# An encoder layer with product-key experts on one core: a second buffer and a shorter period for the seven-product key pairs, attention bias and mask laid out in DRAM, weight splits shared out anew, and another order of the last norm

## The chip, the cores and the metric

The kernel runs on one core of a Trainium2 chip. The metric is device time in microseconds (us) of one execution; the lower the better. Three runs of the kernel before took 979.08, 978.34 and 982.81 us, median 979.08 us. A profile was taken of one more execution.

Engines: PE (TensorE) multiplies matrices out of SBUF into PSUM; DVE (VectorE) and POOL (GpSimd) do elementwise arithmetic; ACT (ScalarE) does activations and copies with a scale; SP (SyncE) issues most DMAs. Each works through its own instructions in a fixed order and waits on semaphores.

## The reference, cut to what matters

One encoder layer on x of 256 tokens by 1024, all in float32:

```
h   = rmsnorm(x) * (1 + sc1) + sh1
[q,k,v | q,k,v] = h @ w_in                    two groups of 8 heads of 64
group A: 2-D neighbourhood attention, learned bias na_rpb, window of 16 columns
group B: three dilated windows, bias -slope[head] * distance, merged by their softmax sums
x   = x + g1 * concat(rmsnorm(oA), rmsnorm(oB)) @ w_out
h2  = rmsnorm(x) * (1 + sc2) + sh2
PEER(h2): q = h2 @ wq; the 16 best of 128 x 128 keys for each of 8 heads, gates = softmax
          y = sum over the chosen (i, j) of gate * gelu(h2 . u[i, j]) * v[i, j]
out = rmsnorm(x + g2 * PEER(h2))
```

u and v are 128 x 128 experts of 1024 numbers: 64 MB each. sh, sc, g come from a product of silu(c) with ada_w.

## The kernel before, in words

**Splits.** A float32 product is made as three products of fp32r parts: a weight tile `raw` (128 x 1024, 512 KB) is loaded by SP (L87), ACT copies its high part `hi` (L96), and DVE or POOL subtracts to get the low part `lo` (L97); then hi·hi, hi·lo and lo·hi are accumulated on PE (`mm3`, L138 to L141). The list `order` (L103 to L120) holds all weight tiles in the order of use, each with a letter: "b" puts its `lo` on POOL, "c" on DVE, "s" is a pair's half that is already in SBUF. `unit()` (L126) hands out the next tile and splits `lead` tiles ahead. `raw`, `hi` and `lo` have a few buffers each, so a load waits until an old tile is used up. WI and WO are the letters of the last eight w_in tiles and of the eight w_out tiles.

**Stages.** (1) Norm, modulation, and the first q, k, v (to about 73 us). (2) Attention (L565 to L596): twelve steps; step i runs one weight tile (V of group B, q and k of group B, then w_out of group A), the scores of head pair i (`att_scores`, L421), the turned probabilities of pair i-1 (`att_turn`) and the values of pair i-2 (`att_values`, L459). For each head and half of the tokens DVE adds the bias and takes the minimum (`st`, L442), ACT takes the exponential (L444), and PE turns it (`pTp`, L453) and multiplies with v (`op`, L466). The bias of group A, `e2s`, is loaded and masked on DVE (L579); that of group B, `dls`, is made from two rows by ACT (L549) and POOL (L550) under the table DLS. Between these DVE sums the modulation (`araw`, L217, `ADA` tells how many pairs of tiles in a step), and at the end w_out of group B and the second norm follow. (3) The queries wq, the scores and the best keys (to about 325 us). (4) `u_chunk` (L661): a tile of u, 24 matmuls of 256 columns, and a Gelu; 36 chunks (AHEAD) while the routing is made, then BESIDE = 92 beside the 64 steps that build the gates (`gp`, L851; `jm` and `gi` on DVE); HOLD is how many of these are left for the last step. (5) The v loop (L1013): for each key i the gated column (`gated`, L879: ACT and DVE write `wx`) times the tile v[i], 4 x 3 matmuls of 512 columns into four PSUM banks `yp`. (6) The last norm (L1045 to L1070).

**Seven products.** Two keys i, i+1 whose index is in `seven` (L115) are taken as one pair: the eight block products (2 keys x 2 halves of tokens x 2 halves of columns) become seven, by Strassen's way in Winograd's form. For that DVE makes sums of the gates (`pair_s`, L928: `sr`, `sx`) and of the weights (`pair_t13`, `pair_t24`, L915 to L922), and splits them (`pair_split`, L924: `sph`, `spl`). `todo` (L1009) says how many places of `plan` ahead of the pair each is done. A pair takes one place of `plan`, so with a distance of 8 keys (SEVEN) there are 6 single keys and a pair in a period. The pair's two raw tiles sit in one buffer `bb` inside GA. At the end `fold` (L997) adds the shared sums to the result.

**What sets the order.** The program is written in the order of the code above, but the order on each engine and on SP's queue is set by the tool that schedules it by its own costs and the buffers; `issue_after` (here on L574, L1062) pins an instruction behind another.

## Time and profile before

| | us |
|---|---|
| median of three runs | 979.08 |
| the profiled execution | 980.62 |
| its span, first to last instruction | 978.8 |
| PE busy | 952.0 |
| DVE busy | 783.5 |
| ACT busy | 565.5 |
| POOL busy | 451.2 |
| from about 74 us to 173 us (attention and second norm) | 99 |
| v loop, first matmul to last | 628.7 to 970.2 |
| last matmul to the end of the span | 8.6 |

The span leaves out 1.8 us of the execution's time. A matmul's busy time is modelled and overlaps the next one's, so PE's busy share says less than the idle times that the timeline puts in brackets, with what ended them. TensorE's clock has two levels, 1.2 and 2.4 GHz; a stretch of the table of windows shows the mean granted, 1.00 being 2.4 GHz.

### The profile page before, as it was taken

What the parts mean: (1) busy time and instruction counts of PE and PEld (TensorE: products, weight loads), DVE (VectorE), ACT (ScalarE), POOL (GpSimd) and SP (SyncE); (2) the same over time, 40 slices, a digit from 0 to 9 for tenths busy, and PEclk for the clock granted to TensorE, in tenths of its full rate; (3) what the DMA queues carried; (4) which work ended last, traced back from release to release, by engine and by line L of the source; (5) the groups of instructions that cost most, each with busy time, mean ns of one, the idle gap of its engine ahead of it and who ended that gap; (6) DMA issues with size and microseconds to landing.
All of it is one profiled execution on the core that took longest, in us unless ns stands there. A gap on an engine that the chain in (4) does not pass through costs nothing.

```text
span 978.8 us, 17367 instructions
## 1 busy us (share of the span) xinstructions
PE 952.0 (97%) x6292; PEld 867.9 (89%) x6292; DVE 783.5 (80%) x1800; ACT 565.5 (58%) x1043; POOL 451.2 (46%) x201
## 2 busy tenths in 40 slices
PE   8899998999999999999999999899999999999996
PEld 5787888999999999999999999888888888888885
DVE  6859888899992677788889887667787888887786
ACT  4366576645445666666666665454655665665653
POOL 2678457677888677777777776300000000000002
PEclk8999799999999999999999999999999999999998
DMA  9776784555554455555545555578657666656562
GB/s 349 284 262 252 260 304 160 160 173 161 184 184 141 152 165 162 170 159 165 164 161 172 155 170 156 177 268 309 222 183 261 235 200 205 195 192 209 158 206 73
DMA packets 53398, 193.76 MB, mean 198 GB/s; under 512 B 5816, under 2 KB 6080, under 8 KB 53184
## 3 DMA queue, kind: packets, MB, share of 16 engines
q1 hardware_dynamic: 52672, 191.59, 59.4%
q8 instruction: 49, 0.80, 0.3%
q10 hardware_dynamic: 576, 1.05, 0.3%
q14 instruction: 37, 0.30, 0.1%
q0 software_dynamic: 64, 0.01, 0.0%
HBM read 190.52 MB, written 2.11 MB: 197 GB/s over the span
## 4 chain that ended last, share of the span: by engine, by line
PE 83%; DVE 3%; issue 2%; ACT 1%; POOL 1%; POOLq 0%; ACTq 0%; DVEq 0%
PE ps L139 15%; PE ps L140 14%; PE ps L141 14%; PE y L140 10%; PE y L139 10%; PE y L141 10%; PE gp L851 3%; PE P L140 1%; DVE araw L217 1%; PE P L139 1%; PE P L141 1%; PE op L466 1%; PE scp L706 1%; ACT hi L96 1%; PE pTp L453 0%
## 5 line engine op out<-in xcount | busy, mean ns | idle before, releaser
L97 POOL TENSOR_TENSOR lo<-raw,hi 128x1024 fp32r<-128x1024 f32 x172 | 422.4, 2459 | 159.1 <-PE ps L141 73.5
L96 ACT ACTIVATE hi<-raw 128x1024 fp32r<-128x1024 f32 x282 | 297.2, 1057 | 187.5 <-issue 63.2
L139 PE MATMUL ps<-h2h,hi 128*128 128x256 f32 x1128 | 320.5, 285 | 3.0 <-DVE GB L868 2.6
L140 PE MATMUL ps<-h2l,hi 128*128 128x256 f32 x1128 | 319.0, 283 | 0.0
L141 PE MATMUL ps<-h2h,lo 128*128 128x256 f32 x1128 | 318.8, 283 | 0.0
L139 PEld LDWEIGHTS ps<-h2h,hi 128*128 128x128 f32 x1128 | 216.2, 192 | 4.1 <-DVE GB L868 3.0
L140 PEld LDWEIGHTS ps<-h2l,hi 128*128 128x128 f32 x1128 | 216.4, 192 | 0.0
L141 PEld LDWEIGHTS ps<-h2h,lo 128*128 128x128 f32 x1128 | 216.2, 192 | 0.0
L97 DVE TENSOR_TENSOR lo<-raw,hi 128x1024 fp32r<-128x1024 f32 x110 | 134.7, 1225 | 53.8 <-issue 44.3
L140 PE MATMUL y<-lo,wx 128*128 128x512 f32 x424 | 165.1, 389 | 0.0
L141 PE MATMUL y<-hi,wx 128*128 128x512 f32 x424 | 165.1, 389 | 0.0
L139 PE MATMUL y<-hi,wx 128*128 128x512 f32 x424 | 165.1, 389 | 0.0
L837 DVE SCALAR_TENSOR_TENSOR gi<-iotaG,iT,gT 128x256 fp32r<-128x256 f32 x256 | 113.8, 476 | 30.5 <-PE gp L851 30.5
L1063 POOL TENSOR_TENSOR GB<-GB 128x512 f32<-128x512 f32 x2 | 2.6, 1290 | 258.3 <-ACT GB L1056 258.3
L141 PEld LDWEIGHTS y<-hi,wx 128*128 128x128 f32 x424 | 79.6, 188 | 16.8
L139 PEld LDWEIGHTS y<-hi,wx 128*128 128x128 f32 x424 | 79.6, 188 | 16.7
L140 PEld LDWEIGHTS y<-lo,wx 128*128 128x128 f32 x424 | 79.6, 188 | 16.5 <-DVE lo L97 0.3
L854 DVE TENSOR_TENSOR gp<-gp,gl 128x512 f32<-128x512 f32 x64 | 44.6, 697 | 8.3 <-ACT gl L853 6.7
L883 ACT ACTIVATE wx<-GB 128x256 fp32r<-128x256 f32 x72 | 28.7, 411 | 36.5 <-PE y L141 36.1
L834 DVE TENSOR_TENSOR jm<-iotaG,jT 128x512 fp32r<-128x512 f32 x64 | 43.6, 681 | 1.6 <-ACT iotaG L823 1.6
L857 ACT ACTIVATE GB<-gp 128x368 f32<-128x368 f32 (+31 forms) x64 | 21.3, 332 | 37.4 <-DVE gp L854 37.4
L989 POOL DMA_DIRECT2D g2d<-g2r x1 | 0.6, 594 | 88.9 <-ACT wxh L943 88.9
(266 smaller groups left out, 1518.0 us busy)
## 6 DMA issues: line engine op xcount, KB each, us to landing
raw<-in_u SPq DMA_DIRECT2D x128, 512.0 KB, 3.5
raw<-in_v SPq DMA_DIRECT2D x106, 512.0 KB, 3.6
araw<-in_ada SPq DMA_DIRECT2D x20, 1024.0 KB, 5.7
raw<-in_w_in SPq DMA_DIRECT2D x24, 512.0 KB, 6.2
GA<-in_v SPq DMA_DIRECT2D x22, 512.0 KB, 4.4
...
```

Of the source, the lines that this page charges most:

```text
L96: nc.scalar.activation(hi, raw, AF.Copy)
L97: ins = eng.tensor_tensor(lo, raw, hi.bitcast(F32), op=OP.subtract)
L139: nc.tensor.matmul(ps, wh, ah, start=first, stop=False)
L140: nc.tensor.matmul(ps, wh, al, start=False, stop=False)
L141: return nc.tensor.matmul(ps, wl, ah, start=False, stop=last)
L217: block_sum.ins = nc.vector.tensor_tensor_reduce(raw, raw, silb, 1.0, init, OP.mult, OP.add, m).ins
L834: nc.vector.tensor_tensor(jm, iotaG[:, None, :].to_broadcast([128, 4, 128]), jT[:, t0:t0 + 4, None].to_broadcast([128, 4, 128]), op=OP.is_ ...
L837: nc.vector.scalar_tensor_tensor(gi[:, t, :, :], iotaG[:, None, :].to_broadcast([128, 2, 128]), iT[:, t0 + t:t0 + t + 1], gT.bitcast(F32)[ ...
L851: nc.tensor.matmul(gp[:, t, :, :], jm[:, t, :], gi[:, t, :, :], start=True, stop=True)
L854: nc.vector.tensor_tensor(gp[:, :, 0, :], gp[:, :, 0, :], gl, op=OP.add)
L857: nc.scalar.activation(GB[:, m:, t0:t0 + 4], gv[:, done:, :], AF.Copy)
L883: nc.scalar.activation(wh, w, AF.Copy)
```

## The change

- **Pairs**: SEVEN's distance goes from 8 keys to 6: 14 pairs for 11. The pair's raw tiles get two rooms in turn, the second one in GA's first cells. The gates' sums are made 4 places ahead (5 before), the weights' sums 3 and 2 (4 and 3 before).
- **u chunks**: BESIDE goes from 92 to 90 and HOLD from 3 to 1. The two chunks left (u[126], u[127]) are run inside the v loop, one behind v[0] and one behind v[1], and their `lo` is made on DVE.
- **Attention**: of the last eight w_in tiles and of the eight w_out tiles every second `lo` is made on DVE. Group B's bias is a table in DRAM of 128 x 3072 (1,536 KB in place of 384 KB), loaded straight into `dls` after step 2, so ACT's and POOL's eight instructions each fall away. Group A's table holds the mask already; DVE's subtraction from the mask becomes a change of sign on ACT. The copy of v's second half and the scaling of the values (`osb`) move from DVE to ACT (the latter in two instructions for one).
- **Last norm**: the gain goes into tiles of its own (`z`), all on DVE and in an order that `then` pins; POOL has only the two powers left. Of the four stores three leave on SP and one on ACT's queue.

```diff
--- before.py
+++ after.py
@@ -23,33 +23,29 @@
-BESIDE = 92
+BESIDE = 90
-HOLD = 3
-SEVEN = (31, 8, 112)
+HOLD = 1
+SEVEN = (31, 6, 112)
-FG0 = (("p", 0, 512), ("p", 512, 1024))
-FG1 = (("v", 0, 512), ("v", 512, 1024))
-SC0 = (("p", 512, 1024), ("a", 0, 512))
-SC1 = (("v", 0, 512), ("a", 512, 1024))
-DLS = (0, 0, 1, 1, 2, 2, 3, 3)
+DLAT = 2
-WI = 'bbbbbbbb'
+WI = 'bcbcbcbc'
-WO = 'bbbbbbbb'
+WO = 'bcbcbcbc'
...
@@ -116,7 +112,9 @@
         plan = [i for i in range(NKEY - LAST) if i - 1 not in seven]
         parts = []
         for i in plan:
-            order += [(p, "s") for p in range(2)] if i in seven else [(v[i], "c")]
+            order += [(seven.index(i) % 2 * 2 + p, "s") for p in range(2)] if i in seven else [(v[i], "c")]
+            if i < NKEY - AHEAD - BESIDE:
+                order.append((u[AHEAD + BESIDE + i], "c"))
         order += [(v[i], "c") for i in range(NKEY - LAST, NKEY)]
         ready = []
...
-                    nc.scalar.activation(v_s[g][:, 0, :], vps[g][0], AF.Copy)
-                    nc.vector.tensor_copy(v_s[g][:, 1, :], vps[g][1])
+                    for T in range(2):
+                        nc.scalar.activation(v_s[g][:, T, :], vps[g][T], AF.Copy)
                         nc.tensor.matmul(op[:, T, :], pts[:, b, T, :], v_s[g][:, b, h * HD:(h + 1) * HD],
-                nc.vector.tensor_tensor(osb[g][:, :, h * HD:(h + 1) * HD], op, ri[:, :, None].to_broadcast([128, 2, HD]),
-                                        op=OP.mult)
+                for T in range(2):
+                    nc.scalar.activation(osb[g][:, T, h * HD:(h + 1) * HD], op[:, T, :], AF.Copy, scale=ri[:, T:T + 1])
...
-            dl = PA.tile([128, 2, 384], F32)
-            nc.sync.dma_start(dl, dil.rearrange("p (a s) -> p a s", a=2))
-            def bias_head(h):
-                nc.scalar.activation(dls[:, h, :], dl[:, 0, :], AF.Copy, scale=2.0 ** -(h + 1))
-                nc.gpsimd.tensor_add(dls[:, h, :], dls[:, h, :], dl[:, 1, :])
-                for h in range(NH):
-                    if DLS[h] == i:
-                        with tc.issue_after(split.pool):
-                            bias_head(h)
+                if i == DLAT:
+                    nc.sync.dma_start(dls, dil.rearrange("p (h s) -> p h s", h=NH))
-                    e3 = e2s[:, 2 * i:2 * i + 2].rearrange("p h s k -> p (h s) k")
-                    nc.vector.tensor_tensor(e3, mask[:, None, :].to_broadcast([128, 12, 64]), e3, op=OP.subtract)
+                    e3 = e2s[:, 2 * i:2 * i + 2].rearrange("p h s k -> p (h s k)")
+                    nc.scalar.activation(e3, e3, AF.Copy, scale=-1.0)
...
-            bb, bt = bl[:, 0:4, :], bl[:, 4:8, :]
-            parts += [bb[:, 3:4, :], bb[:, 0:3:2, :]]
+            bt = bl[:, 4:8, :]
+            rooms = [bl[:, 0:4, :], GA[:, 0:8, :].rearrange("p (b a) t -> p b (a t)", a=2)]
+            for bb in rooms:
+                parts += [bb[:, 3:4, :], bb[:, 0:3:2, :]]
             def pair_load(i):
+                bb = rooms[seven.index(i) % 2]
             def pair_t13(i):
+                bb = rooms[seven.index(i) % 2]
             def pair_t24(i):
+                bb = rooms[seven.index(i) % 2]
...
-                for d, f in ((6, pair_load), (5, pair_s), (4, pair_t13), (3, pair_t24),
+                for d, f in ((6, pair_load), (4, pair_s), (3, pair_t13), (2, pair_t24),
+                if done < NKEY:
+                    ps = u_chunk(done)
+                    nc.scalar.activation(ps[:, :S], ps[:, :S], AF.Gelu)
+                    nc.vector.tensor_mul(cell(done, 0, S), ps[:, :S], cell(done, 0, S))
+                    done += 1
...
+            z = [used(7 + T) for T in range(2)]
+            last = [None]
+            def then(do, *args, **kw):
+                with tc.issue_after(last[0]) if last[0] is not None else nullcontext():
+                    last[0] = do(*args, **kw).ins
+            def gain_of(n):
+                fs = slice(n % 2 * 512, (n % 2 + 1) * 512)
+                then(nc.vector.tensor_mul, z[n // 2][:, fs], ys[n // 2][:, fs], fgb[:, fs])
+            def mean(T):
+                then(nc.vector.tensor_scalar, m[:, T:T + 1], ssq[:, n:n + 1], ssq[:, n + 1:n + 2], EPS, op0=OP.add, op1=OP.add)
+            def scaled(T, f, eng, queue):
+                fs = slice(f * 512, (f + 1) * 512)
+                if eng == "a":
+                    nc.scalar.activation(z[T][:, fs], z[T][:, fs], AF.Copy, scale=r[:, T:T + 1])
+                else:
+                    then(nc.vector.tensor_scalar, z[T][:, fs], z[T][:, fs], r[:, T:T + 1], None, op0=OP.mult)
+                queue.dma_start(out[T * 128:(T + 1) * 128, fs], z[T][:, fs])
+            for n in range(4):
+                T, f = divmod(n, 2)
+                y, fs = ys[T], slice(f * 512, (f + 1) * 512)
+                then(nc.vector.tensor_tensor, y[:, fs], yp[T][f], g2b[:, fs], op=OP.mult)
+                then(nc.vector.tensor_add, y[:, fs], y[:, fs], x1[T][:, fs])
+                nc.scalar.activation(scr[:, fs], y[:, fs], AF.Square, scale=D ** -0.5, accum_out=ssq[:, n:n + 1])
+                if n == 2:
+                    mean(0)
+                if n:
+                    gain_of(n - 1)
+                if n == 2:
+                    for f in range(2):
+                        scaled(0, f, "a", nc.sync)
+            mean(1)
+            gain_of(3)
+            scaled(1, 1, "v", nc.sync)
+            scaled(1, 0, "a", nc.scalar)
...
+    const = np.zeros((128, 256), np.float32)
+    lm = np.log(np.maximum(m, 1.0)).astype(np.float32)
+    mask = np.where(m > 0, -lm, np.float32(BIG))
+    slope = 2.0 ** -np.arange(1, NH + 1)
+    dil = (d[:, None, :] * slope[None, :, None]).astype(np.float32) + mask[:, None, :]
+    return const, dil.astype(np.float32).reshape(128, NH * 384)
+    e2 = np.full((2, 64, NH, 6, 64), -BIG, np.float32)
+            c0 = min(max(cc - 8, 0), 64 - 16)
+            e2[r2, cc, :, :, c0:c0 + 16] = rp[:, 1 - r2:7 - r2, 63 - cc + c0:79 - cc + c0]
```

DVE in the second step of the attention, before. `araw` are the sums of the modulation, `e2s` the bias of group A, `st` and `mn` a score with its bias and its minimum; the rows that follow are the four `st` and `mn` of a head pair.

```order
L217 ISA araw,mod<-araw,silb,col 128x1024
L217 ISA mod 128x1
L217 ISA araw,mod<-araw,silb,col 128x1024
L217 ISA mod 128x1
L217 ISA araw,mod<-araw,silb,col 128x1024
L217 ISA mod 128x1
L579 TENSOR_TENSOR e2s<-cst,e2s 128x768
L456 RECIPROCAL ri<-ri 128x2 x2
L442 ISA st,mn<-sp,e2s 128x256
L442 ISA mn 128x1
```

The same place in the change.

```order
L215 ISA araw,mod<-araw,silb,col 128x1024
L215 ISA mod 128x1
L215 ISA araw,mod<-araw,silb,col 128x1024
L215 ISA mod 128x1
L454 RECIPROCAL ri<-ri 128x2 x2
L93 TENSOR_TENSOR lo<-raw,hi 128x1024
L440 ISA st,mn<-sp,e2s 128x256
L440 ISA mn 128x1
```

One of the three sums goes to a later place, the subtraction on `e2s` is gone, and a weight's `lo` stands ahead of the `st`.

DVE at the turn from the gates to the v loop, before. `gp` and the 128x87x4 row are the last gates, `wx` the first keys' gated columns, `sr` and `sx` the first pair's sums, the 128x256 rows with `ps` (L868, L858 in the change) the products with Gelu of the last u chunks.

```order
L862 TENSOR_TENSOR GB<-gp,GB 128x87x4
L934 TENSOR_TENSOR sr<-GA 128x128
L884 TENSOR_TENSOR wx<-GA,wx 128x256 x3
L868 TENSOR_TENSOR GB<-ps,GB 128x256
L934 TENSOR_TENSOR sr<-GA 128x128
L934 TENSOR_TENSOR sr<-sr,GA 128x128
L934 TENSOR_TENSOR sr<-GA,sr 128x128
L937 TENSOR_TENSOR sx<-sr,sx 128x512
L868 TENSOR_TENSOR GB<-ps,GB 128x256
L97 TENSOR_TENSOR lo<-raw,hi 128x1024
```

The same place in the change.

```order
L852 TENSOR_TENSOR GB<-gp,GB 128x87x4
L929 TENSOR_TENSOR sr<-GA 128x128
L874 TENSOR_TENSOR wx<-GA,wx 128x256
L93 TENSOR_TENSOR lo<-raw,hi 128x1024
L858 TENSOR_TENSOR GB<-ps,GB 128x256
L874 TENSOR_TENSOR wx<-GA,wx 128x256 x2
L929 TENSOR_TENSOR sr<-GA 128x128
L929 TENSOR_TENSOR sr<-sr,GA 128x128
L929 TENSOR_TENSOR sr<-GA,sr 128x128
L93 TENSOR_TENSOR lo<-raw,hi 128x1024
L858 TENSOR_TENSOR GB<-ps,GB 128x256
L932 TENSOR_TENSOR sx<-sr,sx 128x512
```

One `wx` for three stands ahead of the first `ps` product, the other two and the `sr` go behind it, and `lo` of the v loop's tiles come into this stretch (before, the first one is its last row).

DVE in one period of the v loop in the change, from the `lo` of a pair's first sum of weights on.

```order
L93 TENSOR_TENSOR lo<-GA,hi 128x1024
L939 TENSOR_TENSOR wxl<-GB,wxh 128x256 x2
L929 TENSOR_TENSOR sr<-GB 128x128
L929 TENSOR_TENSOR sr<-sr,GB 128x128
L929 TENSOR_TENSOR sr<-GB,sr 128x128
L93 TENSOR_TENSOR lo<-raw,hi 128x1024
L874 TENSOR_TENSOR wx<-GB,wx 128x256
L921 TENSOR_TENSOR spl<-GA,sph 128x1024
L93 TENSOR_TENSOR lo<-raw,hi 128x1024
L921 TENSOR_TENSOR spl<-GA,sph 128x1024
L874 TENSOR_TENSOR wx<-GB,wx 128x256 x2
L93 TENSOR_TENSOR lo<-raw,hi 128x1024 x2
```

Four `lo<-raw` and four `wx` of single keys stand in a period; before there are six of each, beside the same sums and splits of a pair.

## Rows read from the trace of the kernel before

**Rows 1.** The page: busy times, PEclk in 40 slices, the chain that ended last by engine.

```profile
PE 952.0 (97%) x6292; PEld 867.9 (89%) x6292; DVE 783.5 (80%) x1800; ACT 565.5 (58%) x1043; POOL 451.2 (46%) x201
...
PEclk8999799999999999999999999999999999999998
...
PE 83%; DVE 3%; issue 2%; ACT 1%; POOL 1%; POOLq 0%; ACTq 0%; DVEq 0%
```

**Rows 2.** Windows in us: length; busy us (instructions) of each engine; PEclk, DMA share, GB/s.

```profile
73.90:100.40 26.50, 26.10 (x159) 20.39 (x157) 25.07 (x58) 15.58 (x42) 22.86 (x13) 1.00 0.62 238
102.50:113.50 11.00, 10.97 (x51) 10.28 (x52) 9.54 (x25) 6.41 (x17) 5.90 (x2) 0.53 0.77 273
113.96:120.71 6.75, 6.75 (x57) 6.24 (x56) 4.23 (x14) 4.83 (x13) 2.36 (x1) 1.00 0.84 314
121.80:153.00 31.20, 29.29 (x242) 27.44 (x241) 27.09 (x72) 22.29 (x50) 16.94 (x8) 1.00 0.72 270
153.00:173.00 20.00, 17.60 (x139) 16.50 (x139) 15.15 (x21) 12.56 (x27) 16.65 (x11) 1.00 0.54 170
755.26:776.34 21.08, 21.08 (x95) 17.46 (x93) 17.62 (x26) 13.06 (x19) 0.00 (x0) 1.00 0.73 250
```

**Rows 3.** Timeline of DVE in one pair's period: start, us, instruction, [idle before, releaser].

```profile
755.51 1.22 DVE L97 TENSOR_TENSOR lo<-raw,hi 128x1024 fp32r<-128x1024 f32 x1 [0.81 <-issue]
756.65 0.42 DVE L884 TENSOR_TENSOR wx<-GB,wx 128x256 fp32r<-128x256 f32 x1
758.91 1.22 DVE L97 TENSOR_TENSOR lo<-raw,hi 128x1024 fp32r<-128x1024 f32 x1 [1.84 <-issue]
...
773.88 1.23 DVE L97 TENSOR_TENSOR lo<-GA,hi 128x1024 fp32r<-128x1024 f32 x1 [0.78 <-PE y L140]
```

**Rows 4.** Timelines of PE, DVE and POOL at the turn to the v loop.

```profile
617.93 0.39 PE L139 MATMUL ps<-h2h,hi 128*128 128x256 f32 x1 [0.65 <-DVE GB L868]
...
622.97 0.39 PE L139 MATMUL ps<-h2h,hi 128*128 128x256 f32 x1 [1.91 <-DVE GB L868]
...
614.24 3.30 DVE L884 TENSOR_TENSOR wx<-GA,wx 128x256 fp32r<-128x256 f32 x3
...
617.79 2.25 DVE L934 TENSOR_TENSOR sr<-GA 128x128 f32<-128x128 f32 x1
...
614.64 2.62 POOL L97 TENSOR_TENSOR lo<-raw,hi 128x1024 fp32r<-128x1024 f32 x1 [0.47 <-ACT wx L883]
```

**Rows 5.** Timelines of PE and of DVE in the attention's second and third step.

```profile
92.98 1.13 PE L429 MATMUL sp<-k,q 64*128 64x256 f32 x6 [0.40 <-DVE mn L442]
...
102.53 1.48 PE L429 MATMUL sp<-k,q 64*128 64x256 f32 x6 [2.12 <-DVE mn L442]
...
84.41 1.28 DVE L217 CUSTOM_DVE_ANT_0 araw<-araw,silb,col 128x1024 f32<-128x1024 f32 x1
...
99.72 2.40 DVE L217 CUSTOM_DVE_ANT_0 araw<-araw,silb,col 128x1024 f32<-128x1024 f32 x1
```

**Rows 6.** Lines by form, 73.9 to 173 us: count, busy us, mean ns, idle before and releasers.

```profile
L97 POOL TENSOR_TENSOR lo<-raw,hi 128x1024 fp32r<-128x1024 f32 x19 | 49.0, 2589 | 27.5 <-ACT hi L96 20.7 <-issue 3.5 <-PE op L466 2.5
...
L550 POOL TENSOR_TENSOR dls<-dls,dl 128x384 f32<-128x384 f32 x8 | 13.0, 1649 | 0.0
...
L579 DVE TENSOR_TENSOR e2s<-cst,e2s 128x768 f32<-128x768 f32 x4 | 7.6, 1908 | 1.4 <-DMA e2s<-in_e 1.4
...
L468 DVE TENSOR_TENSOR os<-op,ri 128x128 f32<-128x128 f32 x16 | 4.4, 285 | 3.6 <-PE op L466 3.5
```

**Rows 7.** The table of DMA issues: KB each, median us from issue to landing.

```profile
e2s<-in_e SPq DMA_DIRECT2D x1, 1536.0 KB, 9.8
```

**Rows 8.** Timeline of all engines, the last norm.

```profile
969.79 0.39 PE L141 MATMUL y<-hi,wx 128*128 128x512 f32 x1
...
971.46 1.13 DVE L1055 TENSOR_TENSOR GB<-GB 128x512 f32<-128x512 f32 x1
...
973.74 0.95 POOL L1058 TENSOR_TENSOR frs<-fms,half 128x1 f32<-128x1 f32 x1 [0.81 <-DVE fms L1057]
```

More of the change, by code (lines that the diff above doesn't have):

```diff
@@ L151, in body @@
         nc.sync.dma_start(col, cols)
[L152 to L153 removed]
+        cst = P0.tile([128, 256], F32)
+        ident, iota = cst[:, 0:128], cst[:, 128:256]
         ones = P0.tile([128, 128], F32)
@@ L1048, in body @@
             r = WK.tile([128, 2], F32, name="frs")
-            for T in range(2):
-                y = ys[T]
-                n = 2 * T
-                for f in range(2):
-                    fs = slice(f * 512, (f + 1) * 512)
-                    nc.vector.tensor_tensor(y[:, fs], yp[T][f], g2b[:, fs], op=OP.mult)
-                    add = nc.vector.tensor_add(y[:, fs], y[:, fs], x1[T][:, fs])
-                    nc.scalar.activation(scr[:, fs], y[:, fs], AF.Square, scale=D ** -0.5, accum_out=ssq[:, n + f:n + f + 1])
-                nc.vector.tensor_scalar(m[:, T:T + 1], ssq[:, n:n + 1], ssq[:, n + 1:n + 2], EPS, op0=OP.add, op1=OP.add)
-                nc.gpsimd.tensor_tensor(r[:, T:T + 1], m[:, T:T + 1], half[:, 0:1], op=OP.pow)
-                for eng, e0, e1 in FG0 if T == 0 else FG1:
-                    fs = slice(e0, e1)
-                    with tc.issue_after(add.ins):
-                        (nc.gpsimd if eng == "p" else nc.vector).tensor_mul(y[:, fs], y[:, fs], fgb[:, fs])
-                for eng, e0, e1 in SC0 if T == 0 else SC1:
-                    fs = slice(e0, e1)
-                    if eng == "a":
-                        nc.scalar.activation(y[:, fs], y[:, fs], AF.Copy, scale=r[:, T:T + 1])
-                    else:
-                        (nc.gpsimd if eng == "p" else nc.vector).tensor_scalar(y[:, fs], y[:, fs], r[:, T:T + 1], None, op0=OP.mult)
-                    nc.sync.dma_start(out[T * 128:(T + 1) * 128, fs], y[:, fs])
@@ L1073, in constants @@
+            mean(1)
+            gain_of(3)
+            scaled(1, 1, "v", nc.sync)
+            scaled(1, 0, "a", nc.scalar)
 def constants():
     c = np.arange(128)
-    const = np.zeros((128, 320), np.float32)
+    const = np.zeros((128, 256), np.float32)
     const[:, 0:128] = np.eye(128)
     const[:, 128:256] = np.arange(128)
-    c0 = np.clip(c % 64 - 8, 0, 64 - 16)[:, None]
-    kc = np.arange(64)[None, :]
-    const[:, 256:320] = np.where((kc >= c0) & (kc < c0 + 16), 0.0, BIG)
     d = np.abs(np.arange(384)[None, :] - 128 - c[:, None])
@@ L1082, in constants @@
     m = (d <= 64).astype(np.float64) + (d % 4 == 0) + (d % 16 == 0)
-    lm = np.log(np.maximum(m, 1.0))
-    dil = np.stack([d, np.where(m > 0, -lm, BIG)], axis=1).astype(np.float32)
-    return const, dil.reshape(128, 2 * 384)
+    lm = np.log(np.maximum(m, 1.0)).astype(np.float32)
[3 more added lines that the diff above has]
+    return const, dil.astype(np.float32).reshape(128, NH * 384)
```

6 lines of the change are left out of this document (1 added, 5 removed).

## Prediction

> **What bounds the kernel now.** I read the page's busy times and its chain first. TensorE is busy 97% of the span and carries 83% of the chain that ended last [rows 1], so a saving is worth its full size only where it takes away a matmul, an idle time of PE, or a stretch in which PE runs at the lower clock. Second, the windows, one stage at a time [rows 2]: where is PE not full, or not at clock 1.00? Third, the timelines at those places, for what ended each idle time [rows 3 to 5, 8], and the lines by form for the prices [rows 6].
>
> Four places show. In the v loop a period between two pairs takes 21.08 us and PE fills all of it; DVE is busy 17.62 and has waits left. At the turn to the v loop PE stands 0.65 and 1.91 us for DVE's `ps` product. In the attention PE stands 0.40 and 2.12 us for DVE's `mn`, and right behind the longer idle time the clock is 0.53 in the mean for 11 us, that is at the lower level (1.2 GHz) nearly throughout, with PE busy 10.97 of them. From the last matmul to the end of the span lie 8.6 us.
>
> **Pairs.** A pair takes 21 matmuls for the 24 of two single keys. Three more pairs save nine, and PE's list in the new program is indeed nine shorter. A period before has 6 x 12 + 21 = 93 matmuls in 21.08 us, 0.227 each: 9 x 0.227 = **-2.0 us**. This is the surest term, if DVE keeps up. A period now has 4 x 12 + 21 = 69 matmuls, 69 x 0.227 = 15.64 us. DVE's work in it loses two `lo` and two `wx`, by their spacing 1.14 + 0.33 = 1.47 us each pair of them: 17.62 - 2.94 = 14.68 us, 94% of the period. The 3.4 us in which DVE waited (0.81, 1.84 and 0.78 [rows 3]) are mostly those of an engine that is ahead and finds no free buffer; they shrink when it is late, so I count nothing for them. Bounds: none of them stays, or all (the second rival). ACT's 13.06 us fall by two `hi` and two `wx` as well, so it keeps its room. The second room lets the pair's loads start earlier on SP's queue, in which two u tiles also move behind v[0] and v[1]; DMA is busy 73% of a period and a period carries 6 tiles in 15.64 us for 8 in 21.08, the same rate.
>
> **The turn.** DVE's three `wx` take 3.30 us where one takes 0.42 [rows 3, 4], and an `sr` 2.25; both times POOL's `lo` runs beside them (2.62 us from 614.64). The `ps` products behind them come late, and PE stands 0.65 + 1.91. In the new order one `wx` stands ahead of the first `ps` product, and POOL's last two `lo` have become DVE's, so the stretch in which both engines work is shorter. The two late u chunks cost PE the same 48 matmuls, only later; their two `lo` add 2 x 1.14 us to DVE, where v[0]'s and v[1]'s 24 matmuls (5.4 us) and the chunks themselves run beside them. Ends: 0 (the stall stands elsewhere) and -2.56. I take **-2.3**, because order and neighbour are both gone.
>
> **Attention.** Removed from DVE: four subtractions on `e2s`, 7.6 us, and sixteen `os`, 4.4 us [rows 6]. Added: eight `lo` of 1.22 us [rows 3] = 9.8. DVE's sum falls by 2.2 only, but the neighbours change more: POOL loses 13.0 us of `dls` and eight of its `lo`, 8 x 2.59 = 20.7, out of 62. That matters because DVE's sums `araw` take 1.28 us undisturbed and 2.40 in front of the 2.12 us stall [rows 5], and the subtraction 1908 ns in the mean. In the new order a `lo` of 1.22 us stands where one `araw` and one subtraction stood ahead of the four `st`.
>
> - The two idle times: 0.40 + 2.12 = -2.5 (ends 0 and -2.5).
> - The clock: if the 2.12 us stall goes, the 11.00 us after it run at 1.00: 11.00 x (1 - 0.53) = -5.2 (ends 0 and -5.2). In no other window that I list is the clock under 1.00, and the step next to it fills PE (6.75 of 6.75) at 1.00.
> - The idle times left in the later part, 31.20 - 29.29 = 1.9 and 20.00 - 17.60 = 2.4 [rows 2]: I take -1.5, since POOL, with 16.94 and 16.65 us busy there, gives work away; ends 0 and -4.3.
> - New waits: +1.5. A `lo` on DVE waits for its `hi` and its load, with `st` queued behind it, for which ACT's exponentials and then PE wait. ACT takes 32 scalings, two for each `os`; the nearest row is `os` itself, 285 ns, so at most 9.1 us more on an engine that is busy 22.29 of 31.20. Its sign changes treat as many columns (4 x 768) as the eight activations that go (8 x 384). Ends: 0, as the clean step at 113.96 has DVE at 4.23 and ACT at 4.83 of 6.75 us; and 8 x (1.22 + 2.59) = 30, if each `lo` were paid in full with a POOL `lo` ahead of it. I take a value near the clean step, as the program overlaps three head pairs there.
> - Bias of group B from DRAM: 1,536 KB for 384 KB on SP's queue: the size of the `e2s` load, which took 9.8 us to land [rows 7]. `dls` is first wanted in the fifth step, behind 121 us, and the steps before it cover the load: 0. Without that cover it costs up to 9.8.
>
> Together **-7.7**.
>
> **The end.** A DVE addition took 1.13 us for 0.68 while POOL scaled, and POOL's power starts at 973.74, 3.5 us behind the last matmul [rows 8]. With all gains on DVE, ACT's last square waits for ACT's two scalings of the first half; I put the power some 0.8 earlier: **-0.8** (ends -0.3, if ACT is late, and -1.6, if neither is). The fourth store's way on ACT's queue costs or gives little; it lies inside these ends.
>
> **Sum**: -2.0 - 2.3 - 7.7 - 0.8 = -12.8. The profiled execution took 980.62 (span 978.8 and 1.8 around it), so 967.8; the median of the runs is 1.5 lower, hence **966.3 us**. By the four terms' nearer ends the forecast runs from 961 to 971.
>
> **Rivals.**
>
> 1. *The clock falls all the same.* Another stall of some 2 us, now for a `lo` that waits for its load (DMA is busy 0.77 of that stretch), leaves PE at the lower level for as long. For it: DVE is busy 25.07 of 26.50 us before it. Against it: the stall of 1.91 at the turn brought no such fall, as of the page's 40 slices only the one with the attention's stall has a 7 [rows 1]. Then +5.2: 971.5. Chance 0.18.
> 2. *DVE becomes the bound in the v loop* (the slower side). DVE has 15.64 - 14.68 = 0.96 us to spare in a period. If w of its 3.4 us of waits are true ones (for a load, for ACT's `hi`, for the `y` matmul that frees a buffer), a period becomes 14.68 + w, and beyond w = 0.96 each of 13 periods pays the rest: -12.8 + 13 x (w - 0.96). It decides from w = 1.94, where nothing is left of the gain; w = 2.5 gives 966.3 + 13 x 1.54 = 986.3, all 3.4 give 998. For it: one of the three waits was ended by a `y` matmul. Against it: PE, who would have waited, did not stand once in the period. Chance 0.09.
> 3. *The `lo` on DVE meet those on POOL.* Each of the eight then costs a POOL `lo` more, 8 x 2.59 = 20.7 us on DVE, and the attention gains nothing; what is left is -5.1: 974.0. For it: one subtraction in four of 1908 ns in the mean and the 3.30 us for three `wx` show how DVE stands still beside POOL. Against it: DVE's other work is met by POOL just as often now, and POOL works 34 us less. Chance 0.12. The Trainium skill (SBUF — State Buffer, "Who interferes with whom") says that DVE and GpSimd share one pair of ports under an exclusive lock, so that the later one stands still for the whole instruction; that speaks against giving DVE any `lo` while POOL makes others, and the three `wx` in 3.30 us agree with it. The skill (Perfetto Trace Analysis, "Optimizing Scalar/DVE Operations") adds that shifting work between those two may therefore not help.
>
> That the change doesn't do what it says can be left out for the pairs and the bias, as the lists of PE, ACT and POOL show them; for the turn it is the zero end.
>
> **Numbers.** The forecast has 0.61, the rivals 0.18, 0.12 and 0.09. About 0.5% (4.9 us, so 974.2 and 984.0) is what a measurement of this kernel tells from no change. The forecast and most of rival 1 lie below 974.2, rival 3 lies on the border (half and half), rival 2 is a third within and two thirds above: faster 0.61 + 0.13 + 0.05 = 0.79, same 0.05 + 0.07 + 0.03 = 0.15, slower 0.06. The range goes from the forecast's lower end, 961, to 976, which takes in rivals 1 and 3; rival 2 and the tails stay outside.
>
> **What the profile after would show.** Right: a period of 69 matmuls in about 15.6 us with DVE near 14.7; no idle time above 0.5 us on PE at the turn; PEclk 1.00 in every window between 74 and 121 us, and the attention about 92 us long for 99; POOL's `lo` at 162; the power about 2.7 us behind the last matmul. Wrong: PE waiting for DVE's `lo` in every period (rival 2), a window near 0.5 in the attention (rival 1), DVE's new `lo` there at 2 us or more in the mean (rival 3).

## The result, and the profile after

The changed kernel takes 969.56 us in the median of four runs (968.07 to 971.65), the kernel before in the same series 979.91 (978.34 to 982.81). The ratio is 0.9901, 95% interval 0.9885 to 0.9916: faster by 1.0%. The forecast was 966.3 with 961 to 976. The profiled execution took 968.07 (span 966.3) for 980.62, 12.5 us less against 12.8 in the sum.

The page of the changed kernel, its busy times, PEclk in 40 slices and the chain by engine; they answer to [rows 1]:

```profile
PE 942.3 (98%) x6283; PEld 860.3 (89%) x6283; DVE 796.0 (82%) x1820; ACT 578.7 (60%) x1083; POOL 409.7 (42%) x180
...
PEclk9999999999999999999999999999999999999998
...
PE 85%; DVE 4%; issue 4%; POOL 3%; ACT 2%; DMA 1%; SPq 0%; POOLq 0%; ACTq 0%; DVEq 0%
```

PE's busy time fell by 9.7 us, and the slice that had a 7 has a 9. The windows of the changed kernel, one period between two pairs and then the attention with the second norm (us, length, busy time and count of each engine, PEclk, DMA share, GB/s); they answer to [rows 2]:

```profile
750.66:766.30 15.64, 15.64 (x70) 12.96 (x69) 14.55 (x23) 10.19 (x15) 0.00 (x0) 1.00 0.71 237
74.50:97.60 23.10, 22.17 (x148) 18.15 (x148) 18.84 (x56) 16.94 (x52) 2.35 (x1) 1.00 0.79 307
97.60:120.86 23.26, 23.26 (x198) 21.73 (x196) 20.68 (x53) 19.48 (x59) 6.22 (x3) 1.00 0.76 278
120.86:135.00 14.14, 13.65 (x113) 12.37 (x112) 13.94 (x31) 11.86 (x33) 4.75 (x2) 1.00 0.79 291
135.00:150.00 15.00, 12.72 (x98) 11.69 (x98) 14.78 (x26) 9.54 (x19) 7.17 (x4) 1.00 0.63 244
150.00:172.19 22.19, 19.06 (x148) 17.58 (x148) 16.20 (x27) 14.24 (x31) 15.77 (x10) 1.00 0.53 172
```

The period is 15.64 us, full of matmuls. The attention runs at clock 1.00 throughout and PE is full from 97.6 to 120.9. But from 121 to 150 DVE is busy 28.7 of 29.1 us, and PE stands there, mostly for `x_s`, the sum of x and the product with w_out that DVE makes.

To see where the 12.5 us came from, I cut both executions at matmuls whose start the timeline gives: the first score `sp`, the last value product `op`, the first key score `scp`, the last gate product `gp`, the last `y` of the v loop, the end of the span. All runs of this study are in the table (us; the stages are those of each kernel's profiled execution, the last two columns those of its runs, with the ratio to the kernel before in the same series).

| kernel | start to `sp` | `sp` to `op` | `op` to `scp` | `scp` to `gp` | `gp` to last `y` | to the end | median | ratio, 95% interval |
|---|---|---|---|---|---|---|---|---|
| before | 75.8 | 68.4 | 34.9 | 428.9 | 361.9 | 9.0 | 979.9 | |
| the change | 74.5 | 59.5 | 38.2 | 428.9 | 356.8 | 8.4 | 969.6 | 0.9901 (0.9885 to 0.9916) |
| pairs_alone | 74.9 | 66.8 | 34.9 | 429.1 | 361.1 | 9.0 | 977.5 | 0.9987 (0.9972 to 1.0001) |
| turn_alone | 75.0 | 68.4 | 34.9 | 428.9 | 358.6 | 9.0 | 974.4 | 0.9942 (0.9922 to 0.9961) |
| bias_alone | 74.7 | 67.1 | 40.1 | 428.9 | 362.6 | 9.0 | 985.9 | 1.0069 (1.0047 to 1.0091) |
| norm_alone | 74.8 | 65.7 | 34.9 | 429.0 | 363.5 | 8.4 | 979.1 | 1.0001 (0.9987 to 1.0015) |
| w_pool | 74.7 | 59.4 | 38.8 | 428.9 | 357.4 | 8.4 | 969.1 | 0.9898 (0.9879 to 0.9918) |
| wo_pool | 74.9 | 59.4 | 39.5 | 429.7 | 356.6 | 8.4 | 970.0 | 0.9903 (0.9886 to 0.9919) |
| os_dve | 74.5 | 63.3 | 41.8 | 429.4 | 357.4 | 8.7 | 977.7 | 0.9980 (0.9968 to 0.9991) |
| pairs_5 | 74.7 | 60.0 | 38.2 | 429.0 | 354.7 | 8.4 | 966.6 | 0.9883 (0.9852 to 0.9914) |
| os_act_alone | 75.3 | 70.1 | 35.1 | 429.0 | 363.1 | 9.0 | 982.3 | 1.0022 (1.0005 to 1.0040) |
| bias_old | 74.8 | 59.7 | 34.7 | 428.9 | 356.6 | 8.4 | 965.2 | 0.9860 (0.9842 to 0.9877) |
| pairs_5_sums_early | 74.6 | 69.4 | 41.0 | 429.0 | 355.0 | 8.9 | 979.7 | 1.0011 (1.0000 to 1.0023) |
| bias_old_pairs_5 | 74.6 | 59.7 | 34.7 | 429.2 | 354.5 | 8.4 | 962.9 | 0.9823 (0.9810 to 0.9836) |

So the change gave 8.9 us up to the last value product, took back 3.4 behind it, and gave 5.1 from the gates to the end of the v loop and 0.6 at the end. The 1.3 us in front of the first score belong to no edit: there the profiled execution of before is the longest of all fourteen.

### The profile page after: what moved, and what is told of

It reads as the page before. It is cut to its first block, busy times and chain, and to the rows that moved or that the text cites. A ratio compares the mean times of both kernels' runs of the same rounds, so it can differ in the third digit from the quotient of the medians.

```text
span 966.3 us, 17405 instructions
## 1 busy us (share of the span) xinstructions
PE 942.3 (98%) x6283; PEld 860.3 (89%) x6283; DVE 796.0 (82%) x1820; ACT 578.7 (60%) x1083; POOL 409.7 (42%) x180
## 3 DMA queue, kind: packets, MB, share of 16 engines
q1 hardware_dynamic: 52528, 192.48, 59.5%
## 4 chain that ended last, share of the span: by engine, by line
PE 85%; DVE 4%; issue 4%; POOL 3%; ACT 2%; DMA 1%; SPq 0%; POOLq 0%; ACTq 0%; DVEq 0%
PE ps L137 15%; PE ps L139 15%; PE ps L138 15%; PE y L137 10%; PE y L139 10%; PE y L138 10%; PE gp L841 3%; POOL lo L93 2%; PE P L137 1%; PE P L139 1%; PE P L138 1%; DVE lo L93 1%; DVE araw L215 1%; PE scp L696 1%; PE op L464 1%
## 5 line engine op out<-in xcount | busy, mean ns | idle before, releaser
L93 POOL TENSOR_TENSOR lo<-raw,hi 128x1024 fp32r<-128x1024 f32 x162 | 396.9, 2452 | 180.0 <-ACT hi L92 94.7
L92 ACT ACTIVATE hi<-raw 128x1024 fp32r<-128x1024 f32 x276 | 291.3, 1058 | 170.2 <-issue 63.5
L93 DVE TENSOR_TENSOR lo<-raw,hi 128x1024 fp32r<-128x1024 f32 x114 | 147.3, 1301 | 37.3 <-issue 20.1
L138 PE MATMUL y<-lo,wx 128*128 128x512 f32 x400 | 155.8, 390 | 0.0
L137 PE MATMUL y<-hi,wx 128*128 128x512 f32 x400 | 155.8, 390 | 0.0
L139 PE MATMUL y<-hi,wx 128*128 128x512 f32 x400 | 155.7, 389 | 0.0
L139 PEld LDWEIGHTS y<-hi,wx 128*128 128x128 f32 x400 | 75.1, 188 | 16.1
L138 PEld LDWEIGHTS y<-lo,wx 128*128 128x128 f32 x400 | 75.1, 188 | 15.7 <-DVE lo L93 0.2
L137 PEld LDWEIGHTS y<-hi,wx 128*128 128x128 f32 x400 | 75.1, 188 | 15.3
L873 ACT ACTIVATE wx<-GB 128x256 fp32r<-128x256 f32 x66 | 25.9, 412 | 47.0 <-PE y L139 47.0
L921 DVE TENSOR_TENSOR spl<-GA,sph 128x1024 fp32r<-128x1024 f32 x28 | 34.2, 1222 | 11.7 <-ACT sph L920 11.7
```

The source lines that it names most:

```text
L92: nc.scalar.activation(hi, raw, AF.Copy)
L93: ins = eng.tensor_tensor(lo, raw, hi.bitcast(F32), op=OP.subtract)
L137: nc.tensor.matmul(ps, wh, ah, start=first, stop=False)
L138: nc.tensor.matmul(ps, wh, al, start=False, stop=False)
L139: return nc.tensor.matmul(ps, wl, ah, start=False, stop=last)
L873: nc.scalar.activation(wh, w, AF.Copy)
```

## Experiment 1: four parts, each alone on the kernel before

> The kernel before with 14 pairs, two rooms and the later places of the sums, nothing else. Theory (a saving of nine matmuls, nothing else on the path): every period between two pairs takes 69 x 0.2267 = 15.64 us, and from the last gate product to the last matmul of the v loop it takes 361.9 - 2.0 = 359.9 us; the two stalls at the turn to the v loop stay (2.9 us together); the whole some 2.0 us below before. Rival (DVE becomes the bound, or a wait for the pair's loads): periods over 15.64 us, and the gain is smaller than 2.0 or a loss.

```diff
-SEVEN = (31, 8, 112)
+SEVEN = (31, 6, 112)
...
+            rooms = [bl[:, 0:4, :], GA[:, 0:8, :].rearrange("p (b a) t -> p b (a t)", a=2)]
...
-                for d, f in ((6, pair_load), (5, pair_s), (4, pair_t13), (3, pair_t24),
+                for d, f in ((6, pair_load), (4, pair_s), (3, pair_t13), (2, pair_t24),
...
```

All thirteen periods are 15.64 us long, as forecast; no rival showed. The stretch from `gp` to the last `y` fell by 0.8 only. In this execution the clock was at the lower level for 3.4 us behind the 1.91 us stall at the turn, half of which, 1.7, is lost; norm_alone has the same fall there and takes 363.5 us, 1.6 more than before and 2.4 more than pairs_alone. The runs give 0.9987: not told from no change, and fitting 2.0 us.

> The kernel before with two u chunks run inside the v loop and one instead of three left for the last step of the gates, nothing else. Theory (PE stood at the turn for DVE, which stood still beside POOL): the stalls of 0.65 and 1.91 us go, and from the last gate product to the last matmul it takes 361.9 - 2.9 = 359.0 us; the whole 2 to 3 us below before. Rival (the stall goes to another place): no idle time less in sum, 361 to 362 us, the whole within 1 us of before.

```diff
-BESIDE = 92
+BESIDE = 90
-HOLD = 3
+HOLD = 1
...
+            if i < NKEY - AHEAD - BESIDE:
+                order.append((u[AHEAD + BESIDE + i], "c"))
...
+                if done < NKEY:
+                    ps = u_chunk(done)
```

The theory held: 358.6 us, 3.3 less, and the runs say 0.9942. In the changed kernel's timelines of DVE and of POOL at the turn the same is seen; they answer to [rows 4]:

```profile
605.03 2.40 POOL L93 TENSOR_TENSOR lo<-raw,hi 128x1024 fp32r<-128x1024 f32 x1 [2.02 <-PE ps L139]
...
607.51 0.41 DVE L874 TENSOR_TENSOR wx<-GA,wx 128x256 fp32r<-128x256 f32 x1
...
609.31 0.74 DVE L874 TENSOR_TENSOR wx<-GA,wx 128x256 fp32r<-128x256 f32 x2
...
609.98 0.28 DVE L929 TENSOR_TENSOR sr<-GA 128x128 f32<-128x128 f32 x1
```

POOL's last `lo` ends at 607.4, before the first `wx`. One `wx` now takes 0.41 and the next two 0.74 together, where three took 3.30; `sr` takes 0.28 for 2.25. The stalls of 0.65 and 1.91 had cost more than their brackets. By PE's timeline of before, matmuls there start every 0.12 us; from the last one ahead of each stall to the second one behind it 1.15 and 2.42 us pass in place of 0.24, so 0.91 and 2.18 were lost.

> The kernel before with group B's bias loaded as a table from DRAM, nothing else. Theory A (DVE is late in the attention's third step because POOL's eight additions for that bias and its weights' low parts hold it up): the stall of 2.12 us before the scores goes or falls under 1 us, the clock stays at 1.00, and the attention with the second norm (first score to first key score) takes 96 to 97 us for 103.2. Theory B (DVE's own list is too long there, with its sums of the modulation and its bias subtractions): a stall of about 2 us stays, PEclk falls to about 0.5 for some 10 us as before, and the stage takes 102 to 104 us.

```diff
...
-                        with tc.issue_after(split.pool):
-                            bias_head(h)
+                if i == DLAT:
+                    nc.sync.dma_start(dls, dil.rearrange("p (h s) -> p h s", h=NH))
```

Neither theory held whole. The stall before the scores went and the clock stayed up there, as in theory A, yet the stage became 4 us longer, since PE stood at another place. The timelines of PE, POOL and DVE of this kernel show it, in the norm of group A:

```profile
122.77 0.37 PE L477 MATMUL tp<-cst,os 128*128 128x128 f32 x1 [3.93 <-ACT os L492]
...
117.93 2.37 POOL L97 TENSOR_TENSOR lo<-raw,hi 128x1024 fp32r<-128x1024 f32 x1 [5.35 <-ACT hi L96]
120.25 1.71 POOL L177 TENSOR_TENSOR rs<-ms,half 128x2 f32<-128x2 f32 x1
...
118.77 2.61 DVE L217 CUSTOM_DVE_ANT_0 araw<-araw,silb,col 128x1024 f32<-128x1024 f32 x1 [0.49 <-DMA araw<-in_ada]
```

The norm's power `rs` was queued on POOL behind a `lo`, and then took 1.71 us for some 0.7: beside it ran DVE's sum `araw`, which had begun before it and ended at 121.4, and the power ended 0.6 us behind that. ACT's scaling `os` and PE's transposes `tp` waited for it. Behind this stall the clock was at the lower level for 3.4 us, and twice more for as long behind later ones. Freeing POOL moved the stall, it did not remove it.

> The kernel before with the new last norm, nothing else. Theory: the last matmul to the end of the span takes 8.4 us for 9.0 (counted from the matmul's start), the whole 0.6 us below before, too little for the runs to tell. Rival (ACT's scalings hold up the last square, or the store on ACT's queue is late): 9.0 us or more.

```diff
-                for eng, e0, e1 in FG0 if T == 0 else FG1:
...
+            mean(1)
+            gain_of(3)
+            scaled(1, 1, "v", nc.sync)
+            scaled(1, 0, "a", nc.scalar)
```

The end took 8.4 us for 9.0, and the runs can't tell it from no change (1.0001), as expected. In the changed kernel's timeline the power now starts 3.27 us behind the last matmul's start, for 3.95 [rows 8]:

```profile
957.90 0.39 PE L139 MATMUL y<-hi,wx 128*128 128x512 f32 x1
...
961.17 0.93 POOL L1066 TENSOR_TENSOR frs<-fms,half 128x1 f32<-128x1 f32 x1 [2.31 <-DVE fms L1056]
```

This run showed a second thing by the way. Its attention is the one of before, with the same instructions in the same order on PE, DVE, ACT and POOL, and with the same stall of 2.12 us before the scores (PE's timeline), but the clock did not fall. The window around the stall, of norm_alone and of pairs_alone:

```profile
101.52 0.70 PE L429 MATMUL sp<-k,q 64*128 64x256 f32 x4 [2.12 <-DVE mn L442]
...
98.00:112.00 14.00, 11.88 (x90) 10.08 (x88) 13.53 (x35) 9.20 (x24) 8.76 (x4) 1.00 0.82 297
```

```profile
98.00:112.00 14.00, 11.89 (x68) 10.81 (x68) 13.53 (x35) 8.36 (x24) 8.06 (x3) 0.76 0.84 296
```

The same instructions behind the same stall ran at 1.00 in one kernel and at 0.76 in the other (and at 0.53 for 11 us in the profile of before [rows 2]). By the clock's records the lower level lasted 0 us in norm_alone, 6.8 in pairs_alone and 10.2 in before and turn_alone. Half of that, 0, 3.4 and 5.1 us, is what PE lost while it lasted: at its end the matmuls of before lie 4.7 us behind those of norm_alone. But the stage does not pay it all. From the first score to the first key score these kernels take 100.6, 101.7, 103.2 and 103.3 us, so the falls cost 0, 1.1 and 2.7. PE, being ahead without the fall, waits longer further on. PE's timelines of before and of norm_alone at the next idle time:

```profile
125.85 0.44 PE L477 MATMUL tp<-cst,os 128*128 128x128 f32 x2 [0.36 <-ACT pts L455]
```

```profile
122.17 0.44 PE L477 MATMUL tp<-cst,os 128*128 128x128 f32 x2 [1.45 <-ACT pts L455]
```

The runs say the same. Of the 60 runs of the kernel before that stand beside the experiments, the 16 with a mean granted clock of 0.994 take 977.8 us in the mean and the 21 with 0.989 take 980.6: 2.8 us for a clock that is lower by 0.5% of the span, which is 4.9 us.

## Experiment 2: parts taken back from the changed kernel, and more pairs

> The changed kernel with all low parts of the attention's weights on POOL again (both letter lists all b). The changed kernel took 97.7 us from the first score to the first key score, before 103.2. Theory A (the shift of half the low parts to DVE is what the attention's gain needs, since POOL's list is late without it, as in the run with the bias alone): 101 to 107 us, the whole 4 to 9 us above the changed kernel, 973 to 978. Theory B (the shift costs more than it gives: DVE's seven low parts of that stage took 2.16 us each in the mean, and DVE is full from 120 to 150 us): 94 to 97 us, the whole 966 to 969.

```diff
-WI = 'bcbcbcbc'
+WI = 'bbbbbbbb'
-WO = 'bcbcbcbc'
+WO = 'bbbbbbbb'
```

> The changed kernel with the low parts of the w_out tiles alone on POOL again. In the changed kernel DVE is busy 14.78 of 15.00 us from 135 to 150 us and PE stands there for its sums x_s; four low parts of 2.0 to 3.4 us are in that part of DVE's list. Theory A (they are what PE stands for): 95 to 96.5 us for the stage, the whole about 968. Theory B (POOL then is late with them, with its squares and powers queued behind): 98 to 103 us, the whole 970 to 975.

```diff
-WO = 'bcbcbcbc'
+WO = 'bbbbbbbb'
```

Neither run bears out its theories: these two and the changed kernel agree, 969.1, 970.0 and 969.6 us. (wo_pool's 98.9 us for the stage lies inside theory B's range, but its theory does not show: PE stands for no power or square of POOL in it.) From the first score to the last value product they take 59.4, 59.4 and 59.5 us; behind it 0.6 and 1.2 us more, and in both the clock was at the lower level for 3.4 us there, which takes up to 1.7. So no worth of the shift of half the low parts to DVE is seen here. And PE stands for `x_s` also where DVE makes none of them; PE's timeline of w_pool:

```profile
136.85 0.39 PE L137 MATMUL ps<-oTh,hi 128*128 128x256 f32 x1 [2.44 <-DVE x_s L503]
```

> The changed kernel with the scaling of the attention's values on DVE again (16 instructions of about 0.29 us, for 32 on ACT of 0.32 as the trace shows per instruction pair spacing of 0.2). Theory A (DVE is the bound of the attention's second half, so each microsecond put back there is paid): the stage takes 99 to 102 us for 97.7, the whole 971 to 974. Theory B (they hide in DVE's waits for scores): 97 to 98.5 us, the whole within 1 us of the changed kernel.

```diff
-                for T in range(2):
-                    nc.scalar.activation(osb[g][:, T, h * HD:(h + 1) * HD], op[:, T, :], AF.Copy, scale=ri[:, T:T + 1])
+                nc.vector.tensor_tensor(osb[g][:, :, h * HD:(h + 1) * HD], op, ri[:, :, None].to_broadcast([128, 2, HD]),
+                                        op=OP.mult)
```

The attention became 7.4 us longer, more than theory A had, with 4.6 us of work put back. PE stands in the norms of both groups, as in bias_alone, and POOL's power is again behind a `lo` and beside a sum of DVE that had begun before it (`araw`, 114.57 to 117.22). With the two stalls the clock went to the lower level for 3.4 and 6.8 us, which is part of the price. PE's and POOL's timelines of os_dve:

```profile
118.62 0.48 PE L475 MATMUL tp<-cst,os 128*128 128x128 f32 x1 [3.41 <-ACT os L490]
...
147.26 0.69 PE L475 MATMUL tp<-cst,os 128*128 128x128 f32 x2 [3.94 <-ACT os L490]
...
112.72 3.42 POOL L93 TENSOR_TENSOR lo<-raw,hi 128x1024 fp32r<-128x1024 f32 x1 [7.79 <-ACT hi L92]
116.10 1.71 POOL L175 TENSOR_TENSOR rs<-ms,half 128x2 f32<-128x2 f32 x1
```

In the changed kernel POOL's power comes first and takes 0.72:

```profile
113.71 0.72 POOL L175 TENSOR_TENSOR rs<-ms,half 128x2 f32<-128x2 f32 x1 [6.06 <-ACT ms L273]
114.65 3.12 POOL L93 TENSOR_TENSOR lo<-raw,hi 128x1024 fp32r<-128x1024 f32 x1 [0.22 <-ACT hi L92]
```

> The changed kernel with a pair every 5 keys: 17 pairs, three single keys in a period. PE needs 57 x 0.2267 = 12.92 us in a period; DVE was busy 14.55 in a period with four singles, so 14.55 - 1.47 = 13.08 with three. Theory (DVE's waits shrink to nothing when it is late): periods of 13.1 to 13.3 us, 16 x 0.2 to 0.4 lost against 9 x 0.2267 = 2.0 gained, so the whole 1 to 4 us above the changed kernel. Rival (about 1 us of DVE's waits per period are true ones and stay): periods of 14 us and more, the whole over 15 us above it.

```diff
-SEVEN = (31, 6, 112)
+SEVEN = (31, 5, 112)
```

Better than expected: the periods are 12.92 to 12.99 us, PE's own time, and from the last gate product to the last matmul it takes 354.7 us, 2.1 less than the change; nine matmuls are 2.0. The kernel takes 966.6 us in the median, but one of its four runs took 971.2, so the runs alone don't tell it from the change. The windows of two of its periods:

```profile
717.31:730.23 12.92, 12.92 (x58) 10.70 (x57) 12.89 (x22) 8.94 (x13) 0.00 (x0) 1.00 0.74 241
846.54:859.48 12.94, 12.94 (x58) 10.70 (x57) 12.91 (x21) 8.77 (x13) 0.00 (x0) 1.00 0.60 205
```

DVE is busy 12.89 of 12.92 us: none of its waits stays when it has no time for them. Rival 2 is settled, with no room for it even where DVE is filled to the brim.

## Experiment 3: which part carries the attention's gain, and a faster kernel

> The kernel before with the scaling of the attention's values on ACT, nothing else. Putting it back on DVE in the changed kernel cost 7.4 us in the stage from the first score to the first key score (105.1 for 97.7). Theory A (this one step carries the attention's gain, since the norm behind it no longer waits in DVE's queue): the stage takes 97 to 99 us for 103.2, without stalls behind the norm's scaling. Theory B (it gains only together with the freed POOL): 101 to 104 us.

```diff
-                nc.vector.tensor_tensor(osb[g][:, :, h * HD:(h + 1) * HD], op, ri[:, :, None].to_broadcast([128, 2, HD]),
-                                        op=OP.mult)
+                for T in range(2):
+                    nc.scalar.activation(osb[g][:, T, h * HD:(h + 1) * HD], op[:, T, :], AF.Copy, scale=ri[:, T:T + 1])
```

Theory A fell, and theory B's 104 was passed too: 105.1 us, 1.9 more than before. The stall before the scores grew to 3.66 us (PE's timeline), and a fall of the clock followed it:

```profile
95.81 1.54 PE L429 MATMUL sp<-k,q 64*128 64x256 f32 x6 [3.66 <-DVE mn L442]
```

> The changed kernel with group B's bias made by ACT and POOL as before, the rest as changed. Theory A (POOL's 13 us are needed by the norm's powers and by DVE): the stage takes 101 us and more, the whole 972 to 976. Theory B (POOL has room for them, as it had for the eight low parts, whose return cost 0.6 us): 97 to 99 us, the whole 968 to 971.

```diff
-                if i == DLAT:
-                    nc.sync.dma_start(dls, dil.rearrange("p (h s) -> p h s", h=NH))
+                for h in range(NH):
+                    if DLS[h] == i:
+                        with tc.issue_after(split.pool):
+                            bias_head(h)
...
```

This is faster than the change, 965.2 us, below what either theory had, and the gain lies behind the last value product: 34.7 us for 38.2. The same seven low parts on DVE take less there. The lines by form between 74 and 173 us, of the changed kernel and of bias_old:

```profile
L93 DVE TENSOR_TENSOR lo<-raw,hi 128x1024 fp32r<-128x1024 f32 x7 | 15.1, 2161 | 0.4 <-ACT hi L92 0.4
```

```profile
L93 DVE TENSOR_TENSOR lo<-raw,hi 128x1024 fp32r<-128x1024 f32 x7 | 10.4, 1482 | 0.5 <-issue 0.3 <-ACT hi L92 0.2
```

One of them shows how that comes about. DVE's and POOL's timelines near 125 us, the changed kernel first:

```profile
125.16 3.04 DVE L93 TENSOR_TENSOR lo<-raw,hi 128x1024 fp32r<-128x1024 f32 x1
...
124.72 2.39 POOL L93 TENSOR_TENSOR lo<-raw,hi 128x1024 fp32r<-128x1024 f32 x1 [6.95 <-PE pTp L451]
```

```profile
124.94 1.22 DVE L93 TENSOR_TENSOR lo<-raw,hi 128x1024 fp32r<-128x1024 f32 x1
...
125.44 2.96 POOL L93 TENSOR_TENSOR lo<-raw,hi 128x1024 fp32r<-128x1024 f32 x1 [7.48 <-ACT hi L92]
```

In the changed kernel POOL began 0.4 us earlier, and DVE's `lo` ended 1.1 us behind POOL's end at 127.1; in bias_old DVE began first, took 1.22, and POOL paid. The Trainium skill (SBUF — State Buffer, "Who interferes with whom") gives the rule: a DVE instruction with two inputs in SBUF and a GpSimd instruction that reads SBUF want the same ports, and the one that issues first holds them for its whole instruction while the other is blocked. These rows agree with it, down to which engine waits.

Four such low parts take 3.04, 2.94, 2.05 and 3.43 us from 121 to 151 us in the changed kernel, on an engine that is full there, and PE stands for `x_s`; PE's timeline of the changed kernel:

```profile
138.68 0.38 PE L137 MATMUL ps<-oTh,hi 128*128 128x256 f32 x1 [1.00 <-DVE x_s L503]
...
147.12 0.39 PE L137 MATMUL ps<-oTh,hi 128*128 128x256 f32 x1 [0.85 <-DVE x_s L503]
...
152.12 0.66 PE L252 MATMUL xp<-cst,x_s 128*128 128x128 f32 x4 [1.67 <-DVE x_s L503]
```

But they are not what decides this part: w_pool, with none of them on DVE, takes 38.8 us there, no less than the change. What goes with the loss in every case is the table. In the column from `op` to `scp` the seven kernels that load it from DRAM take 38.2 to 41.8 us, and the seven that make the bias on ACT and POOL 34.7 to 35.1, whatever else differs between them. Put into the kernel before (bias_alone) it costs 5.3 us there, in part by the clock; taken out of the change it gives 3.5.

No instruction waits for the table itself: it lands at 82.1 us and is first read at 99.1. But the tool puts its load early on SP's queue, ahead of the first score, and not behind step 2 as the program has it. SP's timelines of the changed kernel and of bias_old:

```profile
65.59 0.34 SPq L83 DMA_DIRECT2D raw<-in_w_in  x1
66.02 0.38 SPq L565 DMA_DIRECT2D dls<-in_dil  x1
...
80.33 0.42 SPq L83 DMA_DIRECT2D raw<-in_w_in  x1
```

```profile
66.13 2.44 SPq L83 DMA_DIRECT2D raw<-in_w_in  x2
```

A weight tile that bias_old loads by 68.6 leaves at 80.3 in the change. And the last of DVE's sums of the modulation comes later, at 142.1 us for 139.0, with four of them behind the last value product for two. DVE's timelines of the two:

```profile
142.11 1.21 DVE L215 CUSTOM_DVE_ANT_0 araw<-araw,silb 128x1024 f32<-128x1024 f32 x1
```

```profile
139.03 1.21 DVE L215 CUSTOM_DVE_ANT_0 araw<-araw,silb 128x1024 f32<-128x1024 f32 x1
```

The table of 1,536 KB also took longer to land than I had from `e2s` [rows 7]. The table of DMA issues of the changed kernel:

```profile
dls<-in_dil SPq DMA_DIRECT2D x1, 1536.0 KB, 16.1
```

So taking the bias from a table is shown as the cause of these 3.5 us. By which way, the loads behind it, the later sums, or the order that the tool then writes, was not taken apart.

> The changed kernel with a pair every 5 keys, and with the sums of the modulation taken earlier in the attention (two pairs of tiles in each of steps 1 to 4, none in the last three, in place of one in each). In the changed kernel PE stands for DVE's x_s from 135 us on, where DVE is full with these sums, while DVE has waits from 74 to 98 us. Theory A (those sums are what x_s waits for): the part from the last value product to the first key score takes 35 to 36.5 us for 38.2, the whole 963.5 to 965.5. Theory B (the loads of the sums' tiles can't come earlier, or the scores wait for them): that part as long, or the part before it longer than 59.5 us; the whole 966 to 971.

```diff
-ADA = (0, 2, 1, 1, 1, 1, 1, 1, 1, 1, 1, 1)
+ADA = (0, 2, 2, 2, 2, 1, 1, 1, 1, 0, 0, 0)
...
-SEVEN = (31, 6, 112)
+SEVEN = (31, 5, 112)
```

Theory A fell by far: 69.4 us for 59.5 up to the last value product, and 41.0 behind it. With more sums in the early steps, PE waited in many small places, for POOL's low parts, ACT's scalings and `x_s`, and the clock fell three times for 3.4 us. No sum is left behind the last value product in this kernel, and that part is still long: the late sums alone are not the table's price. The v loop kept its 355 us.

> The changed kernel with group B's bias made by ACT and POOL as before, and with a pair every 5 keys. The two places are far apart, and the order on DVE through the attention is that of the run bias_old. Theory (the two gains add): the stage from the first score to the first key score takes 94.4 us again, from the last gate product to the last matmul of the v loop 354.7, the whole 962 to 963, less than both kernels. Rival (what an edit does to the attention is chance of a run and not of its order, as with the clock's falls): the stage takes 97 us or more, the whole 965 to 968.

```diff
-SEVEN = (31, 6, 112)
+SEVEN = (31, 5, 112)
...
+                        with tc.issue_after(split.pool):
+                            bias_head(h)
...
```

The two gains add: 94.4 and 354.5 us, 962.9 in all, ratio 0.9823. This kernel beats both, and its five runs lie within 0.8 us of each other (962.69 to 963.46), where before spread over 4.5 and the change over 3.6.

## Why the prediction was right, and where its steps were not

- **Pairs, -2.0.** Right: periods of 15.64 us to the hundredth, DVE at 14.55 for the 14.68 worked out. pairs_alone by itself can't be told from no change; the next nine matmuls less (pairs_5) gave 2.1 in their stage. That DVE's waits before were those of an engine ahead of its buffers was shown by pairs_5; rival 2 fell.
- **The turn, -2.3.** Right in its mechanism, too small: 3.3 alone (turn_alone), 4.0 by the medians. The stalls' full price is 3.1, with the late starts behind them, and I had kept part of it back for a stall elsewhere that did not come.
- **The end, -0.8.** 0.6 in the profiled executions, of the right sign, and too little for the runs to tell. ACT's two scalings do delay the last square, as said.
- **Attention, -7.7.** 5.5 in the profiled executions, and about 4.4 by the medians (an estimate: 10.35 less the 2.0, 3.3 and 0.6 of the others). This is the term of the sum that was mis-sized, and the reasons under it were worse than the sum. The two stalls went (2.5) and the clock stayed at 1.00, as said. But "if the 2.12 us stall goes, the 11.00 us after it run at 1.00" took one execution's fall for the price of the stall, and took all that PE loses in the fall for what the stage loses: 5.2, where kernels with the same attention measured 0, 1.1 and 2.7. Before the last value product the change gained 8.9; less 2.5 and 2.7 that leaves 3.7, for which no term of the sum stands. The later part, for which I took -1.5 and +1.5, became 3.4 us longer. There rival 3's mechanism did happen, at 2161 ns a `lo` for 1221 in the v loop, past the 2 us that the prediction gave as its sign; but only four of seven were hit, and w_pool shows that they do not carry the loss. That these errors met at a sum only 2.2 us off is luck.
- **The load of the table.** "The steps before it cover the load: 0" was the wrong price for that edit. Nothing waits for the table, as said, though it is first read at 99.1 us (105.2 in the kernel before, and not behind 121); yet each kernel that loads it pays some 3.5 us behind the last value product.
- **The neighbours.** I had the freed POOL as the cause of the gain. The runs do not bear it out: the low parts back on POOL changed nothing, and the bias back on ACT and POOL made the kernel faster by 4.3 us.

What carries the attention's gain is not one part. Alone, the bias table (+4.0) and the scaling on ACT (+1.9) both made the stage longer; taken out of the change, the scaling costs 7.4 and the table gains 3.3. What could be shown is where PE stands in each case: before the scores for `mn`, in the norms for a power that stands behind a `lo` and a sum of DVE, or at the end for `x_s`. Each edit moves the tool's order, and with it the stall from one of these places to another. Idle time is not all: against norm_alone, whose clock did not fall either, the same 443 matmuls from the first score to the last value product take 59.5 us for 65.7, with 3.4 less idle and 2.9 less in the time that counts as busy, most of it between the matmuls of the scores `sp`. Why this order has none at the first two was not shown; the subtraction moved to ACT, and the copy of v, were not tried alone, and may carry part of the gain.
